# A trunk of two layers: where the norm's steps stand beside the split of weights and the conditioning work

## The chip, the cores and the metric

One Trainium2 chip, one of its cores. The metric is the device time of one execution in microseconds (us), the median of several runs. The kernel is written in Python on a layer that takes the instructions in the order in which the program issues them, keeps one in-order queue for each engine, and sets all semaphores. The order on an engine is made by that layer's scheduler: of the instructions whose operands and buffers are free by its own estimate, the one issued first by the program goes first. That order is then fixed.

## The reference

The input x has 256 tokens of 2048 values, in float32. Two residual layers follow. In each, a vector c gives six vectors of 2048 (shift, scale and gate for the mixer; the same for the MLP), by a product with a matrix of 2048 x 12288 (adaLN).

```python
for l in range(DEPTH):                                   # DEPTH = 2
    mod = silu(c) @ ada_w[l] + ada_b[l]
    shift1, scale1, gate1, shift2, scale2, gate2 = jnp.split(mod, 6, axis=-1)
    h = _modulate(_rms(x, norm1_g[l]), shift1, scale1)   # h * (1 + scale) + shift
    mix = _even_mixer(h, ...) if l % 2 == 0 else _mla_mixer(h, ...)
    x = x + gate1[:, None, :] * mix
    h = _modulate(_rms(x, norm2_g[l]), shift2, scale2)
    x = x + gate2[:, None, :] * (jnp.square(jax.nn.relu(h @ mlp_w1[l])) @ mlp_w2[l])
```

Layer 0's mixer joins a gated spatial mix and a convolution, and ends in a projection of 2048 x 2048. Layer 1's is a low-rank attention with 16 heads: its input projection has 512 columns for the queries' low rank, 512 for keys and values, and 64 for a shared rotary key; it too ends in a projection of 2048 x 2048. The MLP's matrices are 2048 x 8192 and 8192 x 2048.

## The kernel before, in words

**Tokens and products.** The 256 tokens are two halves of 128, h = 0 and 1. `self.x[h]` holds a half's residual. A product takes the activations as stationary operand, transposed (128 values by 128 tokens), and the weights as moving operand, 512 columns at a time, in float32 split into a high part and a low part: three matmuls for each block of 128 rows (high x high, high x low, low x high). A weight tile is 4 blocks by 512 columns, 1 MB. `wraw` loads it on SyncE's queue into one of four `raw` buffers; `wtile` lets ScalarE cast it to the high part `wh` (three buffers) and VectorE subtract to get the low part `wl` (two buffers) (L94, L95). `gemm_part` runs one tile, half 0 and then half 1 (L183 to L185). With `skew`, `gemm` runs the last two tiles of a product as a pair, all of half 0 ahead of half 1. Products whose input comes from a norm at the MLP go by quarters of the input, four blocks each: `gemm_quarter` and `unit_halves` (L210 to L212) run three column blocks ("units") for one quarter while the norm makes the next; for the first quarter the first two units go as a pair, half 0 of both first.

**The norm.** `residual` adds the gated product to x (L411, L412) and lets ScalarE sum the squares (L340). `x_rstd` turns the sum into 1/rms with some ten operations on one value per token (L345 to L90). `norm_t` scales a quarter of x by it into `xn` (L354) and transposes it on TensorE (L107). `norm_quarter` lets ScalarE scale and shift the transposed blocks into `full` (L380) and VectorE split them into `h_h` (L382) and `h_l` (L383). `norm_start` computes `x_rstd` for both halves before the first quarter. The attention's norm (`norm_mod`) makes all four quarters ahead of its products, and those run by columns: 320, 256 and then 512.

**Conditioning.** The adaLN products of 1 x 2048 by a matrix run on VectorE, beside the rest. They are a queue of steps, each with a 1 MB load through the same four `raw` buffers. A step of a row or a column has one VectorE operation (L297, L237); a step of `ada_quarters` has four (L267, L269). `side_work` is called for each weight tile and takes steps at a rate given with them (`R0` to `R6`, `RA`); with `self.hold` set it takes none. `ada_until` takes steps until a condition holds. After layer 0's mixer has begun, the shift and scale of layer 0's MLP are such a queue: 32 steps in four quarters of eight, the first quarter done by the time of the mixer's output projection; the first four of the other 24 go at rate 2.5, the rest at 0.8 per tile.

**The three places of the change.** At the end of layer 0's mixer (`even`) the output projection's fourth block of columns is an ordinary `gemm`, and side work goes on. At the ends of layer 0's MLP and of the attention, `at_end` sets the pair and the hold. In the attention and in layer 1's MLP `self.first = 2`: the low parts of the first two weight tiles are made by GpSimd instead of VectorE (L95 under POOL). In layer 0's MLP that isn't so, and the hold is off from the start.

`tc.issue_after(ins)`, used before in `even`, lets each instruction of its block that is on `ins`'s engine stand behind `ins` in that engine's order; it adds no semaphore and binds no other engine.

## Time and profile before

| what | value |
|---|---|
| median of 3 runs | 2177.03 us (2175.73 to 2178.15) |
| the profiled execution | 2179.71 us, of which the span of the trace is 2178.0 us |
| TensorE busy | 2081.9 us, 9138 matmuls |
| VectorE busy | 1565.5 us |
| ScalarE busy | 930.8 us |
| GpSimd busy | 147.1 us |
| read from HBM | 564.06 MB |
| mean granted TensorE clock | 0.986 |

Times in the profile count from the start of the span. PE is TensorE's matmuls, DVE VectorE, ACT ScalarE, POOL GpSimd, SPq the instructions that SyncE issues. "out<-in" names the program's tiles, xN counts merged instructions, and a bracket gives the idle time before an instruction with what ended it. In the view by stretches the columns are the stretch, its length, the busy time (and number of instructions) of PE, PE's weight loads, DVE, ACT and POOL, the granted clock, the DMAs' busy share, and GB/s.

### The profile page before, as it was taken

Reading aid. Unit: us, or ns where it says so; the run is one execution under the profiler, and the core shown is the slowest. Engines: PE = TensorE matmul, PEld = TensorE weight load, DVE = VectorE, ACT = ScalarE, POOL = GpSimd, SP = SyncE. Lnnn points to the kernel's source line nnn. Section 1 sums busy time; section 2 is a strip of 40 time slices with the busy share of each in tenths; the row PEclk is TensorE's granted clock in tenths of the full one; section 3 lists DMA queues with packets and bytes.
Section 4 is the critical chain, followed back from the end, with each engine's and each line's share of the span. In section 5 each row is a group of like instructions: output and inputs, shape, how many; then the busy total and the mean of one; then the engine's idle time right before and its main releaser. Section 6 shows DMA issues by size and latency. Waiting matters only on the chain.

```text
span 2178.0 us, 23665 instructions
## 1 busy us (share of the span) xinstructions
PE 2081.9 (96%) x9138; PEld 1633.3 (75%) x9138; DVE 1565.5 (72%) x1763; ACT 930.8 (43%) x1184; POOL 147.1 (7%) x95
## 2 busy tenths in 40 slices
PE   2889999799999999999998999989999999999999
PEld 1344458678888888888888888868888888888887
DVE  6849999888777878878667878766656544554555
ACT  2135435344444334334445687444434433433432
POOL 0038710000000000000001000010000000000000
PEclk9999999899999999999999999989999999999999
DMA  9999978799899899989754756747777556556653
GB/s 349 384 351 325 335 248 289 272 316 335 303 337 328 316 322 328 331 309 342 275 178 155 237 163 231 244 140 255 262 270 263 180 191 187 185 192 193 192 190 121
DMA packets 238620, 567.70 MB, mean 261 GB/s; under 512 B 9150, under 2 KB 17784, under 8 KB 221864
## 3 DMA queue, kind: packets, MB, share of 16 engines
q1 hardware_dynamic: 236288, 562.60, 74.5%
q10 hardware_dynamic: 1564, 2.28, 0.3%
q8 instruction: 72, 1.18, 0.2%
q0 software_dynamic: 656, 1.31, 0.2%
q14 instruction: 40, 0.33, 0.0%
HBM read 564.06 MB, written 2.10 MB: 260 GB/s over the span
## 4 chain that ended last, share of the span: by engine, by line
PE 81%; DVE 10%; DMA 5%; ACT 2%; issue 1%; POOL 0%; SPq 0%; ACTq 0%; DVEq 0%; POOLq 0%
PE mm L183 22%; PE mm L185 22%; PE mm L184 22%; PE mm L153 4%; DMA raw<-in_ada_w 3%; PE trp L107 3%; DVE accq L269 3%; DVE wl L95 2%; DVE cvsq L542 1%; PE mm L211 1%; PE mm L210 1%; PE mm L212 1%; DMA raw<-in_mlp_w 1%; DMA raw<-in_ab_w_out 1%; ACT wh L94 1%
## 5 line engine op out<-in xcount | busy, mean ns | idle before, releaser
L95 DVE TENSOR_TENSOR wl<-raw,wh 128x2048 fp32r<-128x2048 f32 (+2 forms) x312 | 704.8, 2259 | 420.8 <-PE mm L184 318.4
L94 ACT CAST wh<-raw 128x2048 fp32r<-128x2048 f32 (+3 forms) x316 | 596.5, 1888 | 779.8 <-PE mm L185 533.0
L183 PE MATMUL mm<-wh,f_h 128*128 128x512 f32 x1024 | 399.6, 390 | 0.0
L185 PE MATMUL mm<-wh,f_l 128*128 128x512 f32 x1024 | 399.3, 390 | 0.0
L184 PE MATMUL mm<-wl,f_h 128*128 128x512 f32 x1024 | 398.7, 389 | 0.0
L185 PE MATMUL mm<-wh,h_l 128*128 128x512 f32 (+2 forms) x928 | 358.4, 386 | 0.0
L183 PE MATMUL mm<-wh,h_h 128*128 128x512 f32 (+2 forms) x928 | 358.2, 386 | 0.0
L184 PE MATMUL mm<-wl,h_h 128*128 128x512 f32 (+2 forms) x928 | 357.0, 385 | 0.6 <-DVE wl L95 0.6
L185 PEld LDWEIGHTS mm<-wh,f_l 128*128 128x128 f32 x1024 | 192.2, 188 | 40.0
L184 PEld LDWEIGHTS mm<-wl,f_h 128*128 128x128 f32 x1024 | 192.3, 188 | 39.8
L183 PEld LDWEIGHTS mm<-wh,f_h 128*128 128x128 f32 x1024 | 192.2, 188 | 39.0
L184 PEld LDWEIGHTS mm<-wl,h_h 128*128 128x128 f32 x928 | 175.0, 189 | 34.2 <-DVE wl L95 1.1
L185 PEld LDWEIGHTS mm<-wh,h_l 128*128 128x128 f32 x928 | 174.9, 189 | 33.3
L183 PEld LDWEIGHTS mm<-wh,h_h 128*128 128x128 f32 x928 | 175.0, 189 | 32.7
L153 PE MATMUL mm<-raw,x 128*128 128x512 f32 x448 | 198.1, 601 | 1.1 <-ACT x L500 0.6
L269 DVE SCALAR_TENSOR_TENSOR accq<-raw,cT,accq 128x512 f32<-128x512 f32 x210 | 153.9, 750 | 16.0 <-DMA raw<-in_ada_w 12.8
L153 PEld LDWEIGHTS mm<-raw,x 128*128 128x128 f32 x448 | 85.4, 193 | 106.4 <-issue 99.5
L237 DVE SCALAR_TENSOR_TENSOR acc<-raw,cT,acc 128x2048 f32<-128x2048 f32 x60 | 140.8, 2347 | 9.6 <-DMA raw<-in_ada_w 9.5
L297 DVE SCALAR_TENSOR_TENSOR acc<-raw,cT,acc 128x2048 f32<-128x2048 f32 x48 | 112.7, 2347 | 3.1 <-DMA raw<-in_ada_w 3.0
L542 DVE SCALAR_TENSOR_TENSOR cvsq<-yp,convw,cvsq 128x256 f32<-128x256 f32 x240 | 96.0, 478 | 0.0
L303 POOL TENSOR_TENSOR side<-side 128x1024 f32<-128x1024 f32 x32 | 74.7, 2360 | 19.6 <-ACT side L302 19.6
L452 ACT ACTIVATE relu<-mm 128x512 f32<-128x512 f32 x60 | 35.8, 599 | 91.9 <-PE mm L185 83.6
(270 smaller groups left out, 2231.3 us busy)
## 6 DMA issues: line engine op xcount, KB each, us to landing
raw<-in_mlp_w SPq DMA_DIRECT2D x256, 1024.0 KB, 5.7
raw<-in_ada_w SPq DMA_DIRECT2D x192, 1024.0 KB, 5.2
raw<-in_ab_w_in SPq DMA_DIRECT2D x32, 1024.0 KB, 9.7
raw<-in_ab_w_out SPq DMA_DIRECT2D x16, 1024.0 KB, 7.5
raw<-in_mla_w_out SPq DMA_DIRECT2D x16, 1024.0 KB, 5.0
raw<-in_mla_w_ukv SPq DMA_DIRECT2D x8, 1024.0 KB
raw<-in_mla_w_uq SPq DMA_DIRECT2D x8, 768.0 KB, 4.6
raw<-in_mla_w_in SPq DMA_DIRECT2D x4, 1024.0 KB, 7.3
```

Of the source, the lines that this page charges most:

```text
L94: self.nc.scalar.copy(hi, src)
L95: (engine or self.nc.vector).tensor_tensor(lo, src, hi.bitcast(F32), op=ALU.subtract)
L107: self.nc.tensor.transpose(ps[:w, i * P : i * P + s.shape[0]], s, self.ident[: s.shape[0], : s.shape[0]])
L153: self.nc.tensor.matmul(ps[h], x[:, 4 * g + k, h * P : (h + 1) * P], raw[:, k, :], start=g + k == 0, stop=4 * g + k == KB - 1,)
L183: nc.tensor.matmul(o, a, hi[:, i, :nw], start=first, stop=False)
L184: nc.tensor.matmul(o, a, lo[:, i, :nw], start=False, stop=False)
L185: nc.tensor.matmul(o, b, hi[:, i, :nw], start=False, stop=last)
L237: nc.vector.scalar_tensor_tensor(acc, raw, self.cT[:, kb : kb + 1], acc, op0=ALU.mult, op1=ALU.add)
L269: self.last = nc.vector.scalar_tensor_tensor(acc, raw[:, k, :], c, acc, op0=ALU.mult, op1=ALU.add).ins
L297: nc.vector.scalar_tensor_tensor(acc, raw, c, acc, op0=ALU.mult, op1=ALU.add)
L303: nc.gpsimd.tensor_tensor(acc[:, sl], acc[:, sl], prod, op=ALU.add)
L542: nc.vector.scalar_tensor_tensor(o, y, wk, o, op0=ALU.mult, op1=ALU.add)
```

## The change

For half 0 the norm's first steps get a fixed place, by marks: the instructions that make `xn` ("x"), the last `full` ("f") and `h_l` ("l") of a half and quarter are kept, and `behind` puts other instructions after them on the same engine.

- In the last `residual` before a norm, half 0's 1/rms and its first `xn` and transposes are issued before half 1's residual, which stands behind that `xn`. Half 1's 1/rms stands behind half 0's first `h_l`.
- The splits of the first three weight tiles stand behind marks: the first behind `xn` of half 0, the second behind `full` and `h_l` of half 0, the third behind those of half 1, all of quarter 0. They are issued in four pieces each, and all on VectorE; GpSimd has no split any more.
- Layer 0's MLP takes part: the output projection of layer 0's mixer ends in a pair, and side work is held from its first tile until the first quarter of the MLP's products is issued.
- Steps that `ada_until` takes before quarter q stand behind half 1's `h_l` of quarter q - 1; the first step that `side_work` takes after a quarter's products stands behind that of the quarter after.
- The attention's norm goes by quarters like the MLP's, with two units (320 and 256 columns); the third product of 512 columns takes the other PSUM pool.

```diff
 class Trunk:
+    FIRST = [[("x", 0, 0)], [("f", 0, 0), ("l", 0, 0)], [("f", 1, 0), ("l", 1, 0)]]
...
     def wtile(self, w, k0, nk, n0, nw):
...
-        engine = self.nc.gpsimd if self.first else None
-        self.split(raw[:, :nk, :nw], hi[:, :nk, :nw], lo[:, :nk, :nw], engine)
-        self.first = max(0, self.first - 1)
+        with self.behind(*(self.first[0] if self.first else ())):
+            for i in range(nk) if self.first else (slice(0, nk),):
+                self.split(raw[:, i, :nw], hi[:, i, :nw], lo[:, i, :nw])
+        self.first = self.first[1:]
         self.side_work(nk * nw / 2048)
         return hi, lo
+
+    def behind(self, *marks):
+        stack = ExitStack()
+        for m in marks:
+            stack.enter_context(self.tc.issue_after(self.marks[m]))
+        return stack
...
         while self.ada_queue and self.ada_credit >= 1:
             self.ada_credit -= 1
-            self.ada_queue.pop(0)[1]()
+            with self.behind(*self.late):
+                self.ada_queue.pop(0)[1]()
+            self.late = ()
...
     def norm_start(self, layer, which):
...
-        r = [self.x_rstd(h) for h in range(NH)]
+        r0, first = self.begun or (None, None)
+        self.begun = None
+        r = [r0, None] if r0 is not None else [self.x_rstd(h) for h in range(NH)]
...
             for h in range(NH):
-                yield h, self.norm_t(h, q, r[h]), [(S[:, k : k + 1], A[:, k : k + 1]) for k in range(4 * q, 4 * q + 4)]
+                if r[h] is None:
+                    with self.behind(("l", 0, 0)):
+                        r[h] = self.x_rstd(h)
+                ps = first if first is not None and (h, q) == (0, 0) else self.norm_t(h, q, r[h])
+                yield h, ps, [(S[:, k : k + 1], A[:, k : k + 1]) for k in range(4 * q, 4 * q + 4)]
...
-    def residual(self, ps, gate, c, last, part=None):
+    def residual(self, ps, gate, c, last, part=None, ahead=False):
...
         for h in range(NH):
+            with self.behind(*([("x", 0, 0)] if ahead and h else [])):
...
+            if ahead and h == 0:
+                r = self.x_rstd(0)
+                self.begun = r, self.norm_t(0, 0, r)
...
     def mlp(self, layer, last):
...
-        self.first = 2 if layer == 1 else 0
-        self.hold = self.hold and layer > 0
+        self.first = self.FIRST
...
             if q < 4:
-                self.ada_until(lambda: self.quarters.get((layer, 3), 4) > q)
+                with self.behind(*([("l", 1, q - 1)] if q else [])):
+                    self.ada_until(lambda: self.quarters.get((layer, 3), 4) > q)
                 self.norm_quarter(quarter, q, x)
             if q >= AHEAD:
                 units = [(ps, w1, u * 512, 512) for u, ps in enumerate(started)]
                 self.gemm_quarter(units, x, q - AHEAD, 2 if q == AHEAD else 0)
                 self.hold = False
+                self.late = (("l", 1, min(q, 3)),)
...
     def even(self, layer):
...
-                pss.append(self.gemm(cat, 0, wo, 0, KB, c * 512, 512))
-            self.residual(pss[c], self.mod[layer, 2], c, "norm")
+                pss.append(self.gemm(cat, 0, wo, 0, KB, c * 512, 512, self.at_end(True)))
+            self.residual(pss[c], self.mod[layer, 2], c, "norm", ahead=c == 3)
...
     def odd(self, layer):
...
-        x = self.norm_mod(layer, 0)
-        self.first = 2
-        self.hold = False
+        x = self.act_pair(KB, f"h{layer}0")
+        quarter = self.norm_start(layer, 0)
+        self.first = self.FIRST
...
-        p1 = self.gemm(x, 0, win, 0, KB, QR, 320)
+        p1, p2 = self.psum2(), self.psum2()
+        for q in range(4 + AHEAD):
+            if q < 4:
+                self.norm_quarter(quarter, q, x)
+            if q >= AHEAD:
+                units = [(p1, win, QR, 320), (p2, win, QR + 320, 256)]
+                self.gemm_quarter(units, x, q - AHEAD, 2 if q == AHEAD else 0)
+                self.hold = False
+                self.late = (("l", 1, min(q, 3)),)
...
-        pq = self.gemm(x, 0, win, 0, KB, 0, QR)
+        pq = [self.ms.tile([P, 512], F32, tag="ms", name=f"pq{h}") for h in range(NH)]
+        for g in range(0, KB, 4):
+            self.gemm_part(pq, x, 0, win, 0, g, KB, 0, QR)
```

More of the change, by code (lines that the diff above doesn't have):

```diff
@@ L61, in __init__ @@
         self.hold = False
-        self.first = 0
+        self.first = []
+        self.marks = {}
+        self.begun = None
+        self.late = ()
         self.conv_rate = 10
@@ L90, in rsqrt, with split @@
         nc.vector.scalar_tensor_tensor(out, w, 1.5 * 3 / 8, out, op0=ALU.add, op1=ALU.mult)
-    def split(self, src, hi, lo, engine=None):
+    def split(self, src, hi, lo):
         self.nc.scalar.copy(hi, src)
-        (engine or self.nc.vector).tensor_tensor(lo, src, hi.bitcast(F32), op=ALU.subtract)
+        self.nc.vector.tensor_tensor(lo, src, hi.bitcast(F32), op=ALU.subtract)
     def act_pair(self, nkb, name):
@@ L142, in side_work @@
             self.ada_credit -= 1
-            self.ada_queue.pop(0)[1]()
+            with self.behind(*self.late):
+                self.ada_queue.pop(0)[1]()
+            self.late = ()
         for _ in range(min(self.conv_rate, len(self.conv_queue))):
@@ L198, in gemm_quarter @@
                 self.unit_halves(units[u : u + 1], ws[u:], x, q)
+        if paired == len(units):
+            self.unit_halves(units, ws, x, q)
     def unit_halves(self, units, ws, x, q):
@@ L379, in norm_quarter @@
             for i, (b, a) in enumerate(cols):
-                nc.scalar.activation(full[:, i, :], ps[:, i * P : (i + 1) * P], AF.Identity, bias=b, scale=a)
+                full_i = nc.scalar.activation(full[:, i, :], ps[:, i * P : (i + 1) * P], AF.Identity, bias=b, scale=a)
+            self.marks["f", h, q] = full_i.ins
             sl = (slice(None), slice(4 * q, 4 * q + 4), slice(h * P, (h + 1) * P))
             nc.vector.tensor_copy(hi[sl], full)
-            nc.vector.tensor_tensor(lo[sl], full, hi[sl].bitcast(F32), op=ALU.subtract)
-    def norm_mod(self, layer, which):
-        pair = self.act_pair(KB, f"h{layer}{which}")
-        quarter = self.norm_start(layer, which)
-        for q in range(4):
-            self.norm_quarter(quarter, q, pair)
-        return pair
+            self.marks["l", h, q] = nc.vector.tensor_tensor(lo[sl], full, hi[sl].bitcast(F32), op=ALU.subtract).ins
     def gated(self, src, gate, h, c):
@@ L399, in gated @@
         nc.vector.tensor_tensor(xs, xs, t, op=ALU.add)
-    def residual(self, ps, gate, c, last, part=None):
+    def residual(self, ps, gate, c, last, part=None, ahead=False):
         nc = self.nc
         for h in range(NH):
-            t = self.tmp.tile([P, 512], F32, tag="t512", name="rt")
-            xs = self.x[h][:, c * 512 : (c + 1) * 512]
-            src = ps[h]
-            if part is not None:
-                nc.vector.tensor_tensor(t, src, part(h), op=ALU.add)
-                src = t
-            nc.vector.tensor_tensor(t, src, gate[:, c * 512 : (c + 1) * 512], op=ALU.mult)
-            nc.vector.tensor_tensor(xs, xs, t, op=ALU.add)
-            if last == "norm":
-                self.sum_squares(h, c)
-            elif last == "out":
-                nc.scalar.dma_start(self.t["out"][h * P : (h + 1) * P, c * 512 : (c + 1) * 512], xs)
+            with self.behind(*([("x", 0, 0)] if ahead and h else [])):
+                t = self.tmp.tile([P, 512], F32, tag="t512", name="rt")
+                xs = self.x[h][:, c * 512 : (c + 1) * 512]
+                src = ps[h]
+                if part is not None:
+                    nc.vector.tensor_tensor(t, src, part(h), op=ALU.add)
+                    src = t
+                nc.vector.tensor_tensor(t, src, gate[:, c * 512 : (c + 1) * 512], op=ALU.mult)
+                nc.vector.tensor_tensor(xs, xs, t, op=ALU.add)
+                if last == "norm":
+                    self.sum_squares(h, c)
+                elif last == "out":
+                    nc.scalar.dma_start(self.t["out"][h * P : (h + 1) * P, c * 512 : (c + 1) * 512], xs)
+            if ahead and h == 0:
+                r = self.x_rstd(0)
+                self.begun = r, self.norm_t(0, 0, r)
     def mlp(self, layer, last):
@@ L464, in mlp @@
                 if fb == DFF // FB - 1:
-                    self.residual(ps, self.mod[layer, 5], c, last, (lambda h: y(h, c)) if c < 3 else None)
+                    self.residual(ps, self.mod[layer, 5], c, last, (lambda h: y(h, c)) if c < 3 else None, c == 3 and last == "norm")
                     continue
@@ L860, in odd @@
             ps = self.gemm((oh, ol), 0, wout, 0, KB, c * 512, 512, self.at_end(c == 3))
-            self.residual(ps, self.mod[layer, 2], c, "norm")
+            self.residual(ps, self.mod[layer, 2], c, "norm", ahead=c == 3)
     def setup(self):
```

5 lines of the change are left out of this document (2 added, 3 removed).

## The prediction

> **What bounds the kernel now.** First the page: busy time, then the chain that ended last.
>
> ```profile
> span 2178.0 us, 23665 instructions
> PE 2081.9 (96%) x9138; PEld 1633.3 (75%) x9138; DVE 1565.5 (72%) x1763; ACT 930.8 (43%) x1184; POOL 147.1 (7%) x95
> ...
> PE 81%; DVE 10%; DMA 5%; ACT 2%; issue 1%; POOL 0%; SPq 0%; ACTq 0%; DVEq 0%; POOLq 0%
> ```
>
> TensorE is busy 96% of the span and carries 81% of the chain. No matmul is removed, so only time in which TensorE waits or runs at a low clock can go. The stages view (busy time by stretch; the clock stands ahead of the DMA share) shows where that is after the start: at the three hand-overs from a residual to the next norm.
>
> ```profile
> 410.00:420.00 10.00, 2.40 (x12) 1.69 (x11) 9.10 (x27) 5.05 (x6) 0.00 (x0) 0.72 1.01 355
> 450.00:460.00 10.00, 10.00 (x45) 8.28 (x45) 10.00 (x13) 1.92 (x1) 0.00 (x0) 1.00 0.77 247
> 480.00:490.00 10.00, 8.26 (x29) 6.29 (x29) 8.06 (x5) 5.00 (x5) 0.00 (x0) 0.83 0.97 370
> 1150.00:1160.00 10.00, 5.76 (x26) 4.50 (x24) 8.87 (x13) 3.25 (x4) 5.80 (x2) 0.93 0.31 76
> 1440.00:1450.00 10.00, 1.87 (x9) 1.21 (x7) 9.83 (x7) 3.04 (x2) 8.18 (x2) 0.76 0.43 120
> 1450.00:1460.00 10.00, 7.84 (x28) 6.29 (x29) 8.01 (x20) 5.73 (x16) 0.00 (x0) 0.55 0.23 92
> ```
>
> TensorE runs 45 matmuls in a full 10 us (the 450 us row): 0.222 to 0.227 us each, I use 0.225. At 410, 1150 and 1440 us (layer 0's MLP, the attention, layer 1's MLP) TensorE works 2.4, 5.8 and 1.9 of 10 us, and the clock falls as well. In layer 0 VectorE and the DMAs are near full in the same stretch (9.1 of 10 us, share 1.01); at 1440 us the DMAs have room (0.43). That difference decides my sum. The timeline of layer 1's MLP:
>
> ```profile
> 1438.67 0.16 DVE L345 TENSOR_REDUCE v<-ssq 128x1 f32<-128x4 f32 x1 [0.79 <-ACT junk L340]
> 1439.15 9.04 POOL L95 TENSOR_TENSOR wl<-raw,wh 128x2048 fp32r<-128x2048 f32 x2 [35.51 <-PE mm L185]
> 1439.24 4.51 DVE L79 SCALAR_TENSOR_TENSOR nr<-r,v 128x1 f32<-128x1 f32 x1
> ...
> 1441.48 0.39 PE L185 MATMUL mm<-wh,o_l 128*128 128x512 f32 x1
> ...
> 1443.78 4.42 DVE L87 SCALAR_TENSOR_TENSOR nr<-nr 128x1 f32<-128x1 f32 x1
> ...
> 1450.71 1.09 PE L107 MATMUL trp<-ident,xn 128*128 128x128 f32 x4 [8.85 <-DVE xn L354]
> ...
> 1450.96 0.16 DVE L345 TENSOR_REDUCE v<-ssq 128x1 f32<-128x4 f32 x1 [0.39 <-ACT junk L340]
> 1451.53 0.22 DVE L79 SCALAR_TENSOR_TENSOR nr<-r,v 128x1 f32<-128x1 f32 x1
> ...
> 1452.61 0.48 DVE L354 TENSOR_SCALAR xn<-x,r 128x512 f32<-128x512 f32 x1
> 1453.38 0.43 DVE L382 CAST h_h<-full 128x512 fp32r<-128x512 f32 x1 [0.28 <-ACT full L380]
> 1453.98 0.78 PE L210 MATMUL mm<-wh,h_h 128*128 128x512 f32 x1
> ```
>
> The last attention matmul ends at 1441.48 + 0.39 = 1441.87; the first MLP matmul starts at 1453.98: 12.1 us. In the first rsqrt two one-element steps take 4.51 and 4.42 us while GpSimd makes the first two low parts (9.04 us); in the second rsqrt, with GpSimd idle, the same L79 takes 0.22. Whatever the mechanism, the first half's chain loses 8.5 us to GpSimd's work.
>
> **The change, part by part.** Prices: VectorE's groups between 412 and 461 us (busy us, then mean ns of one), and the page's row of adaLN loads (KB, us to landing).
>
> ```profile
> L269 DVE SCALAR_TENSOR_TENSOR accq<-raw,cT,accq 128x512 f32<-128x512 f32 x27 | 19.6, 750 | 0.1
> L95 DVE TENSOR_TENSOR wl<-raw,wh 128x2048 fp32r<-128x2048 f32 x6 | 13.8, 2292 | 2.6 <-PE mm L211 1.6 <-ACT wh L94 0.9
> L383 DVE TENSOR_TENSOR h_l<-full,h_h 128x512 fp32r<-128x512 f32 x6 | 4.1, 687 | 0.0
> ...
> raw<-in_ada_w SPq DMA_DIRECT2D x192, 1024.0 KB, 5.2
> ```
>
> *Low parts to VectorE, the first half's norm ahead (layer 1's MLP).* Undisturbed, the chain from the sum (1450.96) to xn (1452.61) takes 1.65 us. From 1438.67 that puts xn at 1440.3 to 1440.8, before the last matmul. The transposes then start at 1441.9. From transposes to first matmul it is 1453.98 - 1450.71 = 3.3 us; that is with transposes at the half clock (1.09 us), so less is possible; but ScalarE may take the other half's square first. I take 3.3: first matmul at 1445.2, gain 8.8 (bounds: 7.5, and 12.1 if nothing were left).
>
> What the gain must pay. Each of the first two low parts now costs VectorE four pieces, 2.3 to 2.8 us by the L95 and L383 rows (2.29 whole, 4 x 0.69 in pieces); the first lies in its wait for transposes and ScalarE (3.3 us), costing nothing; uncovered it would be 2.8 at most. The second half's rsqrt, before done ahead of the first matmul, now stands behind the first half's low part: 0.69 + 1.65 + 0.48, up to 2.8 of second-tile pieces between, then 3.3 to its matmul: 6 to 9 us, against 24 matmuls of the first half (5.4) plus their half-clock time (1.7). I charge 1.0. The second tile's casts now wait behind ScalarE's modulate of the first half; TensorE has 12 matmuls (2.7 us) before it needs them: covered, at most 1 if not. The second half's residual now waits for xn, which is ready (1440.8) before that half's last matmul: no cost. The half clock: before, TensorE ran from 1453.98 to about 1459 at 0.55; the new idle is shorter, and I charge one low stretch of 3.4 us (the 480 us row: clock 0.83 in 10 us behind a short wait) against about 5, worth +1.0. Net: 8.8 - 1.0 + 1.0 = **8.8 us gained**, bounds 6 and 11.
>
> *The attention.* Same construction, smaller.
>
> ```profile
> 1152.85 2.73 DVE L79 SCALAR_TENSOR_TENSOR nr<-r,v 128x1 f32<-128x1 f32 x1
> ...
> 1155.25 0.51 PE L793 MATMUL sc<-mask,identr 128*128 128x384 f32 x2
> ...
> 1164.21 0.61 PE L183 MATMUL mm<-wh,h_h 128*128 128x320 f32 x1
> ...
> 1197.03 0.28 PE L185 MATMUL mm<-wh,h_l 128*128 128x256 f32 x1
> ```
>
> TensorE is free at 1155.25 + 0.51 = 1155.8 and restarts at 1164.2, 8.4 us. With 3.3 it restarts at 1159.1: 5.1 gained. The two projections (320 and 256 columns) now go together by quarter, the same 192 matmuls; but the first half of a quarter is only 24 short matmuls (1164.2 to 1197.3 for 192 and the work between: 0.17 each at most), 4.1 together, so the second half, 6 us behind, is waited for: -1.9; the half clock costs as before. The third projection's accumulators move to other banks, and its loads stay in place: nothing, covered by matmuls on both sides; two mask matmuls (0.51) fall behind it: the same work later. **3.2 gained**, bounds 0.5 and 5.5.
>
> *Layer 0's MLP: the norm ahead, and work held back.* Here the hand-over is alike:
>
> ```profile
> 398.61 0.63 PE L107 MATMUL trp<-ident,accq 128*128 128x128 f32 x4 [1.35 <-DVE accq L269]
> ...
> 404.32 0.69 DVE L221 TENSOR_REDUCE mod<-trp 128x4 f32<-128x512 f32 x1
> ...
> 411.90 0.39 PE L185 MATMUL mm<-wh,cat_l 128*128 128x512 f32 x1
> ...
> 419.89 0.45 PE L107 MATMUL trp<-ident,xn 128*128 128x128 f32 x1 [7.60 <-DVE nr L87]
> ...
> 423.24 0.79 PE L210 MATMUL mm<-wh,h_h 128*128 128x512 f32 x1 [2.26 <-DVE h_h L382]
> ...
> 432.71 0.69 DVE L383 TENSOR_TENSOR h_l<-full,h_h 128x512 fp32r<-128x512 f32 x1
> ...
> 440.25 5.81 SPq L118 DMA_DIRECT2D raw<-in_ada_w  x3
> ...
> 450.17 0.37 SPq L118 DMA_DIRECT2D raw<-in_mlp_w  x1
> ...
> 452.87 5.39 DVE L269 SCALAR_TENSOR_TENSOR accq<-raw,cT,accq 128x512 f32<-128x512 f32 x8
> ...
> 461.51 0.47 PE L210 MATMUL mm<-wh,h_h 128*128 128x512 f32 x1
> ...
> 499.92 0.40 PE L212 MATMUL ms<-wh,h_l 128*128 128x512 f32 x1
> ```
>
> 412.3 to 423.2 is 10.9 us. The last output projection becomes paired, so its first half ends 24 matmuls (5.4 us) ahead instead of 12, and side work is held. The adaLN transposes and the wait before them (398.61: 1.35 + 0.63, and a second four) leave this projection; it ends near 410, and the first MLP matmul comes near 413.5: 9.7 earlier.
>
> But the held work is needed soon. The queue holds 24 adaLN steps for this norm after the mixer (a 1 MB load and four VectorE operations each); from its rates (2.5 for four, then 0.8 a tile) 13 are done before the last projection and 16 after: the reduce at 404.32 closes the sixteenth. Now steps 14 to 16 wait for the first group of tiles and for the second half's low part of quarter 1; they, 17 and 18, and 19 to 24 must pass before quarter 3's norm, and on the load queue quarter 2's first tile comes behind step 24. That order is visible: three loads at 440.25, then the tile's at 450.17; steps to 458.3; its matmuls at 461.51.
>
> The first quarter's two halves plus quarter 1's take about 12 us from the first matmul (before: 423.2 to 433.4, the second half's rsqrt already done), so steps may begin at 426. From there to quarter 2's first low part: 44 operations of 0.67 (5.39 / 8, overlapped) to 0.75 us = 29.6 to 33.0; four low parts, 8.8 to 9.2; a norm quarter, 2 x (0.48 + 0.43 + 0.69) = 3.2; two reduces 1.5. Together 43 to 47: quarter 2 starts at 469 to 473, I take 470, against 461.5, although TensorE would be ready near 450 (two quarters of 72 x 0.225, transposes and a low-clock stretch from 413.5). From there before took 500.3 - 461.5 = 38.8; now the loads are ahead: 2 x 72 x 0.225 = 32.4, 16 transposes at half of 1.09 for four 2.2, one low-clock stretch 1.7: 36.3, end 506.3. **6.0 us lost**, bounds 16 lost and 8.5 gained (next part). Steps that follow are paced by tiles and fall due later: no cost. On SyncE's queue three adaLN loads fall behind the MLP's first tiles, which come sooner for it; GpSimd's queue only loses work; at both layer-1 stages the side work was held before as well, and nothing is queued anew.
>
> *Sum.* 2179.71 (the profiled execution) - 8.8 - 3.2 + 6.0 = 2173.7. That execution lies 2.7 above the median 2177.03, so I predict **2171.0 us**. Outside these stages every matmul keeps its place, so the shift lasts to the end.
>
> **The rivals.**
>
> *Short gaps keep the clock.* The 480 us row speaks against it: TensorE lacks only 1.7 us there, and the clock went to 0.83. If gaps of some 2 us leave it at 1.0, the low stretches (1.7 each) go: 2166. The Trainium skill, "TensorE: Matmul & The Clock Gate", Part 1, states that the clock halves after at least one idle window of about 3.4 us, and by that the new gaps would keep it. By that rule the sum would be 2166; the 480 us row disagrees with it.
>
> *The backlog is hidden.* If quarter 2's tiles get past the late steps, quarter 3 alone waits, near 481 (before: in the 480 us row), ending at 499: 1 gained, 2164; with VectorE's gaps used as well nearly the whole lead stays, 8.5 gained: 2156.5. For it: the DMAs stand at 0.77 in the 450 us row. Against: the load order above, and VectorE at 10.00 in the same row.
>
> *The second halves come late.* If the pieces, the square and the rsqrt of the second half get in each other's way for 2.5 to 3 us more at both layer-1 stages, those bring 6 and 0.5: 2176.5, no change.
>
> *Slower: the backlog waits for loads.* A load takes 5.2 us from issue to landing and there are four buffers. If a step costs 4 to 5 us instead of 2.9, quarter 2 starts at 482 to 493, the loss is 18 to 29, and the time 2183 to 2194. It decides from 3.8 us a step on (a loss above 16.4 cancels 12.0 and the 0.2%). Against it: 1 MB at the 370 GB/s of the 480 us row is 2.8 us.
>
> **How the numbers follow.** 0.2%, about what a measurement tells from no change, is 4.4 us: faster is below 2172.7. Chances: forecast 0.45 (its own range 2166 to 2176), clock kept 0.08, backlog hidden 0.19, second halves late 0.16, slower 0.12. Faster: 0.35 of the forecast, 0.08 and 0.19: 0.62. Same: 0.10 and 0.16: 0.26. Slower: 0.12. The range 2158 to 2179 leaves out the slower case and the end of the hidden one.
>
> **What would show it.** In the new trace: no GpSimd operation at both layer-1 hand-overs, each rsqrt step about 0.2 us, xn of the first half before the last matmul; from last to first matmul 3 to 4 us at all three; then in layer 0 TensorE idle some 15 to 20 us before quarter 2, behind adaLN steps, and quarter 2's first matmul near 470. If TensorE starts quarter 2 before 462, the step on the backlog is wrong and the time nearer 2158; if the layer-1 gaps stay above 6 us, the steps on the chain are.

## The result, and the profile after

The change makes the kernel slower by 0.65%: 2191.56 us (median of 6 runs, 2189.63 to 2196.11) against 2177.59 (6 runs, 2175.73 to 2180.19) on the same chip, a ratio of 1.0065, 95% interval 1.0054 to 1.0075. The forecast was 2171.0. The profiled executions differ by 11.7 us (spans of 2189.7 and 2178.0), the medians by 14.0; the stages below are of the former. The page of the changed kernel, its span, busy times and the shares of the chain that ended last:

```profile
span 2189.7 us, 23705 instructions
...
PE 2085.0 (95%) x9138; PEld 1634.1 (75%) x9138; DVE 1562.8 (71%) x1794; ACT 932.3 (43%) x1211; POOL 132.4 (6%) x91
...
PE 84%; DVE 9%; DMA 4%; ACT 2%; issue 1%; SPq 0%; ACTq 0%; DVEq 0%
```

The page can't tell what happened: the same 9138 matmuls, VectorE no busier, 11.7 us more span. So the span is cut where TensorE's last matmul of each stage ends (read from the timeline of each kernel; us):

| kernel | layer 0's mixer ends | layer 0's MLP | attention | layer 1's MLP |
|---|---|---|---|---|
| before | 412.3 | 743.1 | 286.5 | 731.5 |
| after | 410.5 | 759.8 | 289.8 | 725.1 |
| after less before | -1.8 | +16.7 | +3.3 | -6.4 |

Those four differences are the 11.7 us, within rounding.

**Layer 0's MLP.** First the view by stretches, of before and then of after (columns as in the prediction):

```profile
390.00:400.00 10.00, 8.65 (x41) 6.92 (x40) 9.78 (x12) 2.53 (x3) 0.00 (x0) 1.00 0.72 241
400.00:410.00 10.00, 10.00 (x47) 8.14 (x46) 9.93 (x14) 3.83 (x2) 0.00 (x0) 1.00 1.00 362
420.00:430.00 10.00, 7.74 (x30) 6.15 (x31) 7.58 (x18) 4.51 (x12) 0.00 (x0) 0.60 0.64 208
```

```profile
390.00:400.00 10.00, 10.00 (x46) 8.29 (x45) 5.00 (x5) 3.68 (x5) 0.00 (x0) 1.00 0.66 190
400.00:410.00 10.00, 10.00 (x46) 8.29 (x45) 5.62 (x15) 2.56 (x6) 0.00 (x0) 1.00 0.42 145
410.00:420.00 10.00, 5.22 (x16) 3.97 (x16) 7.64 (x21) 4.18 (x10) 0.00 (x0) 0.71 0.31 107
420.00:430.00 10.00, 10.00 (x49) 8.17 (x49) 7.58 (x15) 6.37 (x16) 0.00 (x0) 0.94 0.32 105
...
460.00:470.00 10.00, 1.12 (x4) 0.72 (x4) 9.68 (x15) 0.00 (x0) 0.00 (x0) 0.60 1.03 377
470.00:480.00 10.00, 6.52 (x20) 5.06 (x21) 7.28 (x11) 3.41 (x5) 1.80 (x1) 0.54 0.97 348
480.00:490.00 10.00, 8.06 (x30) 5.95 (x29) 7.79 (x7) 7.00 (x7) 0.00 (x0) 0.83 0.66 208
...
1460.00:1470.00 10.00, 5.13 (x16) 3.34 (x14) 7.64 (x22) 4.18 (x10) 0.00 (x0) 0.83 0.41 117
```

From 390 to 430 us VectorE was busy for 36.4 of 40 us before (with the 9.10 of the row shown in the prediction) and for 25.8 after; the DMAs moved 11.7 MB and now 5.5. From 460 us on TensorE all but stands still (1.12 of 10, the granted clock at half from 462.1 to 479.2) while the other two catch up. How much they have to catch up, in VectorE's groups of instructions (count, busy us, mean ns), from 427.1 us to each kernel's own start of quarter 2, of after and then of before:

```profile
L286 DVE SCALAR_TENSOR_TENSOR accq<-raw,cT,accq 128x512 f32<-128x512 f32 x42 | 29.8, 747 | 0.5
...
L284 DVE TENSOR_SCALAR accq<-raw,cT 128x512 f32<-128x512 f32 x2 | 1.0, 478 | 0.0
```

```profile
L269 DVE SCALAR_TENSOR_TENSOR accq<-raw,cT,accq 128x512 f32<-128x512 f32 x19 | 13.6, 750 | 0.1
```

44 operations for 19: 17.2 us of VectorE that lay before 427 and now lie behind it. The timeline of after:

```profile
408.91 0.49 DVE L371 TENSOR_SCALAR xn<-x,r 128x512 f32<-128x512 f32 x1
...
410.29 0.60 PE L112 MATMUL trp<-ident,xn 128*128 128x128 f32 x4
...
415.67 0.80 PE L227 MATMUL mm<-wh,h_h 128*128 128x512 f32 x1 [4.78 <-DVE h_h L406]
...
444.09 16.47 SPq L123 DMA_DIRECT2D raw<-in_ada_w  x6
...
453.33 16.57 DVE L286 SCALAR_TENSOR_TENSOR accq<-raw,cT,accq 128x512 f32<-128x512 f32 x23
...
462.43 0.37 SPq L123 DMA_DIRECT2D raw<-in_mlp_w  x1
...
468.50 1.12 PE L112 MATMUL trp<-ident,accq 128*128 128x128 f32 x4 [9.71 <-DVE accq L286]
...
470.56 1.90 ACT L99 CAST wh<-raw 128x2048 fp32r<-128x2048 f32 x1 [20.02 <-DMA raw<-in_mlp_w]
...
473.62 1.20 PE L227 MATMUL mm<-wh,h_h 128*128 128x512 f32 x2
```

`xn` is ready ahead of the last matmul and TensorE starts the MLP 7.6 us earlier than before (423.24). Then 23 adaLN operations run without a break, quarter 2's first tile stands in the load queue behind the loads of six adaLN steps (it is issued at 462.43, and ScalarE can cast it at 470.56), and TensorE waits 9.71 us. Quarter 3 ends at 514.65; before it was 500.31.

**The attention.** Its hand-over shrank from 8.8 to 4.6 us, and the third projection (the queries') starts 38.4 us after the MLP's end (41.7 before). Behind it, in the timeline of after:

```profile
1233.63 0.16 DVE L684 TENSOR_SCALAR rss<-rss 128x2 f32<-128x2 f32 x1
...
1233.84 2.35 DVE L254 SCALAR_TENSOR_TENSOR acc<-raw,cT,acc 128x2048 f32<-128x2048 f32 x1
...
1237.68 0.75 DVE L694 TENSOR_SCALAR lxn<-pq,rr 128x512 f32<-128x512 f32 x1
1238.34 2.28 DVE L100 TENSOR_TENSOR wl<-raw,wh 128x2048 fp32r<-128x2048 f32 x1
1240.54 0.74 DVE L694 TENSOR_SCALAR lxn<-pq,rr 128x512 f32<-128x512 f32 x1
...
1241.34 1.11 PE L112 MATMUL trp<-ident,lxn 128*128 128x128 f32 x4 [2.03 <-DVE lxn L694]
```

`rss` is the queries' sum of squares and `lxn` their scaled values. An adaLN step of 2.35 us stands between the sum and its rsqrt, and the split of a weight tile (2.28 us) has come between the two halves' `lxn`. TensorE waits 3.0 us for `lxn` in two waits, the granted clock is at half from 1240.3 to 1247.2, and the eight pairs of heads (from the end of the third projection to the start of the output projection) take 126.2 us instead of 118.3.

**Layer 1's MLP** gained 6.4. Its hand-over:

```profile
1458.45 0.49 DVE L371 TENSOR_SCALAR xn<-x,r 128x512 f32<-128x512 f32 x1
...
1459.83 0.60 PE L112 MATMUL trp<-ident,xn 128*128 128x128 f32 x4
...
1462.58 0.63 ACT L357 ACTIVATE junk<-x 128x512 f32<-128x512 f32 x1 [5.82 <-DVE x L430]
...
1463.21 1.49 ACT L403 ACTIVATE full<-trp,mod,A 128x128 f32<-128x128 f32 x4
...
1465.21 0.50 PE L227 MATMUL mm<-wh,h_h 128*128 128x512 f32 x1 [4.78 <-DVE h_h L406]
```

The transposes are done at 1460.4, yet ScalarE begins the modulate at 1463.21: half 1's square stands ahead of it in ScalarE's queue and waits for half 1's residual. Between last and first matmul lie 5.2 us (12.1 before).

### The profile page after: what moved, and what is told of

It reads as the page before. It is cut to its first block, busy times and chain, and to the rows that moved or that the text cites. A ratio compares the mean times of both kernels' runs of the same rounds, so it can differ in the third digit from the quotient of the medians.

```text
span 2189.7 us, 23705 instructions
## 1 busy us (share of the span) xinstructions
PE 2085.0 (95%) x9138; PEld 1634.1 (75%) x9138; DVE 1562.8 (71%) x1794; ACT 932.3 (43%) x1211; POOL 132.4 (6%) x91
## 3 DMA queue, kind: packets, MB, share of 16 engines
q10 hardware_dynamic: 1564, 2.28, 0.3%
## 4 chain that ended last, share of the span: by engine, by line
PE 84%; DVE 9%; DMA 4%; ACT 2%; issue 1%; SPq 0%; ACTq 0%; DVEq 0%
PE mm L198 22%; PE mm L199 22%; PE mm L200 22%; PE mm L168 5%; DMA raw<-in_ada_w 4%; DVE accq L286 3%; PE trp L112 3%; DVE wl L100 2%; DVE cvsq L564 1%; PE mm L229 1%; PE mm L228 1%; PE mm L227 1%; PE ms L227 1%; PE ms L229 0%; PE ms L228 0%
## 5 line engine op out<-in xcount | busy, mean ns | idle before, releaser
L100 DVE TENSOR_TENSOR wl<-raw,wh 128x2048 fp32r<-128x2048 f32 (+3 forms) x343 | 714.5, 2087 | 422.2 <-PE mm L199 318.0
L198 PE MATMUL mm<-wh,h_h 128*128 128x512 f32 x832 | 326.3, 392 | 0.0
L200 PE MATMUL mm<-wh,h_l 128*128 128x512 f32 x832 | 325.8, 392 | 0.0
L199 PE MATMUL mm<-wl,h_h 128*128 128x512 f32 x832 | 324.4, 390 | 0.0
L200 PEld LDWEIGHTS mm<-wh,h_l 128*128 128x128 f32 x832 | 156.2, 188 | 32.2
L199 PEld LDWEIGHTS mm<-wl,h_h 128*128 128x128 f32 x832 | 156.3, 188 | 31.8
L198 PEld LDWEIGHTS mm<-wh,h_h 128*128 128x128 f32 x832 | 156.3, 188 | 31.2
L227 PE MATMUL mm<-wh,h_h 128*128 128x512 f32 (+2 forms) x192 | 73.2, 385 | 16.4 <-DVE h_h L406 13.7
```

What stands on the lines that cost most here:

```text
L100: self.nc.vector.tensor_tensor(lo, src, hi.bitcast(F32), op=ALU.subtract)
L198: nc.tensor.matmul(o, a, hi[:, i, :nw], start=first, stop=False)
L199: nc.tensor.matmul(o, a, lo[:, i, :nw], start=False, stop=False)
L200: nc.tensor.matmul(o, b, hi[:, i, :nw], start=False, stop=last)
L227: nc.tensor.matmul(o, a, hi[:, i, :nw], start=k == 0, stop=False)
```

## The experiments

All ran as single kernels on one chip per group; a ratio is to the kernel before on that chip. Stage times in us are from each kernel's one profiled execution. Layer 1's MLP as changed is in eleven of them; ten took 724.7 to 727.8 and att_credit 730.1, so a stage is good to some 2 us. The profiled execution of mlp1_only lies 5.2 us above the median of its five runs. The expectations count from before's 2177.6 us; where a group's median of before was another, a ratio times 2177.6 is the fair number.

| kernel | ratio, 95% interval | mixer ends | layer 0's MLP | quarter 2 starts, quarter 3 ends | attention (heads) | layer 1's MLP |
|---|---|---|---|---|---|---|
| before | 1 | 412.3 | 743.1 | 461.5, 500.3 | 286.5 (118.3) | 731.5 |
| after | 1.0065, 1.0054 to 1.0075 | 410.5 | 759.8 | 473.6, 514.7 | 289.8 (126.2) | 725.1 |
| l0_hold_off | 0.9967, 0.9955 to 0.9979 | 412.4 | 740.7 | 458.4, 498.9 | 282.5 (118.5) | 726.0 |
| l0_undone | 0.9979, 0.9970 to 0.9988 | 410.3 | 743.2 | 460.1, 497.0 | 282.0 (118.6) | 727.8 |
| mlp1_only | 0.9960, 0.9946 to 0.9974 | 412.5 | 744.3 | 463.0, 501.7 | 283.5 (118.0) | 725.5 |
| att_credit | 1.0095, 1.0080 to 1.0110 | 410.9 | 758.8 | 473.6, 515.7 | 288.3 (124.8) | 730.1 |
| att_entry | 1.0041, 1.0027 to 1.0055 | 410.1 | 762.4 | 473.5, 515.2 | 282.8 (118.5) | 726.4 |
| half_ops | 1.0016, 1.0005 to 1.0026 | 411.0 | 751.1 | 470.0, 507.8 | 289.4 (126.0) | 724.7 |
| half_loads | 1.0045, 1.0030 to 1.0060 | 409.7 | 757.5 | 469.9, 513.1 | 286.7 (123.5) | 726.5 |
| half_both | 1.0009, 0.9998 to 1.0020 | 410.8 | 753.3 | 469.6, 506.0 | 288.7 (124.8) | 725.0 |
| tile_first2 | 1.0056, 1.0039 to 1.0072 | 409.4 | 756.7 | 456.9, 512.5 | 290.2 (126.2) | 724.8 |
| tile_first_half | 1.0024, 1.0013 to 1.0036 | 409.2 | 752.8 | 458.8, 507.2 | 288.6 (124.7) | 724.8 |
| sq_behind | 0.9934, 0.9920 to 0.9947 | 411.9 | 739.7 | 455.7, 497.6 | 281.0 (118.6) | 725.9 |
| hold_later | 0.9933, 0.9920 to 0.9945 | 412.2 | 739.0 | 456.8, 496.9 | 280.7 (118.6) | 722.2 |
| pieces | 0.9938, 0.9924 to 0.9951 | 411.1 | 744.1 | 458.5, 500.1 | 279.9 (118.5) | 722.4 |
| pieces_l0_undone | 0.9934, 0.9922 to 0.9947 | 410.5 | 743.4 | 460.3, 498.9 | 279.9 (118.6) | 721.8 |

**Which part loses.** l0_hold_off takes one thing out of the changed kernel:

```diff
-                pss.append(self.gemm(cat, 0, wo, 0, KB, c * 512, 512, self.at_end(True)))
+                pss.append(self.gemm(cat, 0, wo, 0, KB, c * 512, 512, True))
```

> The changed kernel without one thing: in layer 0 the adaLN steps are no longer held back while the last output projection and the MLP's first tiles run. The first half's norm still has its fixed place, the last two tiles are still paired, the first tiles' low parts still come in pieces. Theory A (the loss is the hold): VectorE stood at 5.0 and 5.6 of 10 us and the DMAs at 190 and 145 GB/s in the two stretches from 390 us, and what was left out there came back in front of quarter 2; without the hold quarter 2 starts before 465 us (now 473.6), the layer 0 MLP's quarters end near 500 (now 514.5), and since the side work's credit at the attention's start is then 0.25 again instead of 0.40, no adaLN step falls into the query's rsqrt: 2160 to 2168 us. Rival B (the fixed places and the pairing themselves cost it): quarters still end after 510 us, and only the attention changes: 2183 to 2188 us. Rival C (neither, the two losses are of other causes): within 3 us of 2191.6.

Its stretches:

```profile
400.00:410.00 10.00, 9.90 (x46) 7.71 (x45) 8.78 (x14) 4.81 (x7) 0.00 (x0) 1.00 1.01 367
410.00:420.00 10.00, 5.59 (x21) 4.09 (x20) 9.67 (x28) 4.20 (x11) 0.00 (x0) 0.82 0.64 230
420.00:430.00 10.00, 8.78 (x38) 6.84 (x38) 8.26 (x21) 3.61 (x11) 0.00 (x0) 0.84 0.77 259
```

Theory A holds in each stage it named (quarter 2 at 458.4, quarter 3's end at 498.9, heads 118.5); the time, 0.9967 of before or 2170.4, is 2 us above its range and far from B's. VectorE and the DMAs are at work through the hand-over, and the hand-over is as short as with the hold (417.4 less 412.4, 5.0 us; 5.2 with it): the hold is not what makes the chain quick. What it brings is an earlier end of the mixer, by some 1.4 us on average: 409.2 to 411.0 in the eight kernels with the hold, 410.3 to 412.5 in the eight without. The attention is right as well without being touched. l0_undone takes layer 0's part back whole (`ahead`, the pair, the marks and the hold), and mlp1_only the attention's part too:

> The changed kernel with layer 0's part taken back whole: no hold, no pairing, no fixed place and whole low parts at layer 0's MLP; the attention and layer 1's MLP as changed. Theory A: layer 0's MLP loses its 14.8 us; the attention, with its credit at 0.25, keeps the 3.3 us that it has gained when the query projection starts and loses none of the 7 us after; layer 1's MLP keeps 6.9: 2177.6 - 3.3 - 6.9 = 2167.4 us, 2164 to 2171. Rival D (the attention's own loss of 7 us comes from its new order of projections or the query's accumulators in the other banks, not from where the side work falls): the attention still ends 3.8 us later than before, relative to its start: 2177.6 + 3.8 - 6.9 = 2174.5 us.

> Layer 1's MLP alone as changed (first half's norm ahead, fixed places, low parts in pieces on VectorE); layer 0 and the attention as before, except that the attention's first two low parts are on VectorE too, in whole tiles and with no fixed place. If the terms are independent: 2177.6 - 6.9 = 2170.7 us for the MLP, and at the attention up to 2.7 us more from the rsqrt step that no longer takes 2.73 us: 2168 to 2171. If the MLP's gain in the changed kernel was helped by what came before it, above 2173.

By its ratio l0_undone is at 2173.0, outside A's range and nearer to D's 2174.5 than to A's 2167.4; the stage decides between the two, 282.0 for the attention and not 290. mlp1_only, at 2168.9, is where it was expected: its MLP gained 6.0, and the attention 3.0, where all that differs from before is that the first two splits run on VectorE and no longer on GpSimd beside the first half's rsqrt (the step of 2.73 us on L79 and one of 2.81 on L87 take 0.22 and 0.16 there). So of the 3.7 to 4.5 that the attention gains in the kernels with its part and a credit of 0.25 (l0_hold_off, l0_undone, att_entry), about 3 seem to need no new order at all; with a stage good to some 2 us, this is one profile's figure.

**Why the attention lost.** Two tries at the side work's credit (a number that grows with each weight tile; a step is taken when it passes 1). By the program's own count it is 0.25 at the attention's start before, and 0.40 with the hold in layer 0. att_credit raises it by 0.425 after the paired projections, att_entry lowers it by 0.15 at the start:

> The changed kernel with one number more: after the attention's paired projections the side work's credit is raised by 0.425, so that the steps fall after the same tiles of the query projection as before; the work and its amount stay. Layer 0 keeps its loss. Theory A': no 2.35 us adaLN step between the query's squares and its rsqrt (now at 1233.8 us), the transposes for both halves come within 6 us of the projection's end (now 9.4), the attention gains about 6 to 7 us: 2191.6 - 6.5 = 2185 us, 2183 to 2187. Rival D (the order of projections or the banks cost it): the step moves and the attention stays as long, within 2 us of 2191.6.

> The changed kernel with one number more: the side work's credit is lowered by 0.15 at the attention's start, from 0.40, which the hold in layer 0 has left, to the 0.25 that it has without the hold. Layer 0 keeps its loss. VectorE's order in the attention is then that of the kernel without the hold. Theory A'' (the attention's loss is where the steps fall in its heads, and that is set by the credit): the attention takes 282.5 us as it does without the hold (289.8 as changed), the heads 118.5 (126.2): 2191.6 - 7.3 = 2184 us, 2182 to 2187. Rival D' (what slows the heads is the later side work's amount or the memory traffic after a late layer 0): heads stay above 123 us, 2189 to 2196.

The first missed: by its ratio 2198.3 us, above both ranges. The rsqrt was freed (the first matmuls of the queries' second projection came 6.7 us after the third projection's end, as before, against 10.0), but the heads still took 124.8 us, with one wait alone of 2.53 us at 1333.4. So the step in the rsqrt is not the whole of the loss; that the other steps fell badly is argued from this. The second gave 118.5 and 282.8, as l0_hold_off has, and by its ratio 2186.5, in its range. In its timeline only the rsqrt's own operations, of 0.16 to 0.17 us each, stand between VectorE's sum of squares and `lxn`:

```profile
1236.51 0.16 DVE L684 TENSOR_SCALAR rss<-rss 128x2 f32<-128x2 f32 x1
...
1238.29 1.41 DVE L694 TENSOR_SCALAR lxn<-pq,rr 128x512 f32<-128x512 f32 x2
```

So the new order of projections and the other banks cost nothing that the stage shows; 0.15 more in a counter, left by the hold a whole MLP earlier, cost 7 us.

**What paces the refill in layer 0.** The changed kernel with half of the VectorE operations, half of the loads, or both, in the 11 late steps alone. The lines are those of half_both; half_ops changes the last of them only, half_loads the load only, and its four operations read the loaded half twice:

```diff
+            less = layer == 0 and j0 == 3 and 8 * q + 2 * g + i >= 21
-            raw = self.wraw(self.t["ada_w"][layer], 4 * g, 4, (j0 + i) * D + q * 512, 512)
+            raw = self.wraw(self.t["ada_w"][layer], 4 * g, 2 if less else 4, (j0 + i) * D + q * 512, 512)
-            for k in range(4):
+            for k in range(2 if less else 4):
```

> The changed kernel, with only two of the four VectorE operations in each of the 11 adaLN steps of layer 0 that the hold leaves for the MLP; their loads stay whole. (Half of their products are left out.) VectorE has 22 operations less of 0.72 us, 16 us. Theory V (VectorE sets the pace of the refill): quarter 2's first matmul comes 12 to 16 us earlier, near 460 (now 473.6), and the time is 2191.6 - 12 to 16 = 2176 to 2180 us. Theory L (the loads set it: 377 GB/s in the stretch from 460 us): quarter 2 starts after 470, 2188 to 2191. Both at once: near 466, 2183 to 2186.

> The changed kernel, with only half of each load (512 KB for 1024) in the same 11 adaLN steps; all four VectorE operations stay and read the loaded half twice. (The second half of the products is replaced.) 5.8 MB less, at 377 GB/s 15.3 us of the DMAs. Theory V: quarter 2's first matmul still after 470, 2188 to 2191 us. Theory L: near 460, 2176 to 2180. Both at once: near 466, 2183 to 2186.

> The changed kernel, with both halvings: in the 11 late adaLN steps of layer 0 two of four VectorE operations and half of each load. (Half of their products are left out.) With half the operations alone quarter 2 started at 470.0 and ended at 491.4, VectorE at 6.8 and 6.4 of 10 us and the DMAs at 370 and 397 GB/s; with half the loads alone it started at 469.9, VectorE at 10.00 twice. If the refill is bound by the two together and by nothing else, quarter 2 starts at 456 to 461, quarter 3 ends at 495 to 501 (before: 500.3), and layer 0's MLP takes 740 to 745 us: 2174 to 2178 us. If something else of the hold (the tiles parked in the load buffers, the order of loads) is left, quarter 2 starts after 465 and the time is above 2181.

The stretches from 450 to 470 us of half_ops, and then of half_loads:

```profile
450.00:460.00 10.00, 10.00 (x46) 8.29 (x45) 6.79 (x8) 0.00 (x0) 0.00 (x0) 1.00 1.02 370
460.00:470.00 10.00, 3.75 (x16) 2.48 (x15) 6.39 (x12) 1.95 (x2) 1.44 (x1) 0.72 1.04 397
```

```profile
450.00:460.00 10.00, 7.40 (x33) 5.76 (x31) 10.00 (x14) 0.00 (x0) 0.00 (x0) 1.00 0.67 206
460.00:470.00 10.00, 1.26 (x5) 0.86 (x5) 10.00 (x17) 1.90 (x1) 0.00 (x0) 0.58 0.85 278
```

VectorE looks like the tighter of two bounds that lie close together: without half of its work quarter 3 ends 6.9 us earlier, and then the DMAs are full (share 1.02 and 1.04); without half of the loads 1.5 us, with VectorE at 10.00. No one theory's number came out, and both halvings together gave 8.6 and not the whole. What was left looked like the place of quarter 2's first tile in the load queue, behind six adaLN loads (half_both, SyncE's queue):

```profile
442.36 14.17 SPq L123 DMA_DIRECT2D raw<-in_ada_w  x6
...
457.88 0.37 SPq L123 DMA_DIRECT2D raw<-in_mlp_w  x1
```

So quarter 2's first tiles (two in tile_first2, one in tile_first_half, where both are halved) were loaded ahead:

```diff
-        raw = self.wraw(w, k0, nk, n0, nw)
+        raw = self.early.pop(0) if self.early else self.wraw(w, k0, nk, n0, nw)
...
+                if layer == 0 and q == 3:
+                    self.early = [self.wraw(w1, 8, 4, u * 512, 512) for u in range(2)]
                 with self.behind(*([("l", 1, q - 1)] if q else [])):
                     self.ada_until(lambda: self.quarters.get((layer, 3), 4) > q)
```

> The changed kernel with its hold, and quarter 2's first two tiles loaded and split ahead of the last adaLN steps: on the load queue they pass five adaLN loads, on VectorE 18 operations; no work is left out. Theory O (a part of the loss is that the tiles stand behind the late steps, in the load queue and on VectorE): quarter 2 starts at 459 to 464 us (now 473.6), its first 48 matmuls run under the steps, and quarter 3, which needs the last step, ends at 501 to 507 (now 514.65): 2191.6 - 8 to - 13 = 2179 to 2184 us. Rival P (the end is set by the last step alone, quarter 3's norm): quarter 2 starts early, but quarter 3 ends after 511, 2188 to 2191.

> The kernel with half the operations and half the loads in the late steps (so half of their products are left out), and quarter 2's first tile ahead of five of the adaLN loads. With the two halvings quarter 2 still started at 469.63 and quarter 3 ended at 506.0, since its first tile was issued behind six adaLN loads, at 457.88. Theory O: quarter 2 at 458 to 463, quarter 3's end at 497 to 502, layer 0's MLP 743 to 748 us (753.3), and with that all of the loss is accounted for. If quarter 3 still ends after 505, something of the hold is left that neither the operations, the loads nor this order explains.

Theory O fell. Quarter 2 starts at 456.9 and 458.8, as early as it could, and quarter 3 ends only 2.1 us earlier in the one and no earlier in the other: TensorE's wait moves behind the last step (5.61 us at 468.4 in tile_first2, and the clock halves for 20.5 us from 472.4). Rival P is right for the most part: the last step sets the end, whatever runs ahead of it. One more queue stands on the way: ScalarE casts quarter 2's remaining tiles behind quarter 3's modulate, which waits for the last step (ScalarE is idle for 20.06 us ahead of it in tile_first2 and for 16.56 in tile_first_half), and TensorE then waits 4.8 us for these tiles in either, most of it at the half clock (3.1 us in l0_hold_off, at full clock). No run moved these casts, so what they cost is not shown. Without the hold layer 0's loss is gone (shown). Halving VectorE's late operations gives back 6.9 of the 14.3 us (shown); halving the loads 1.5, which is less than a stage is good to; the other 6 us stay unassigned.

**What was left of the hand-over.** On l0_hold_off, the square of half 1 behind half 0's modulate on ScalarE; then, in hold_later, layer 1's hold kept until the norm's four quarters are made; then, in pieces, the first cast in four parts; last, pieces with layer 0's part taken back:

```diff
                 if r[h] is None:
+                    with self.behind(("f", 0, 0)):
+                        self.sum_squares(h, 3)
                     with self.behind(("l", 0, 0)):
                         r[h] = self.x_rstd(h)
...
-                if last == "norm":
+                if last == "norm" and not (ahead and h):
                     self.sum_squares(h, c)
...
-                self.hold = False
+                self.hold = layer == 1 and q < 4
...
+            for i in range(4) if (h, q) == (0, 0) else (slice(0, 4),):
```

> The kernel without layer 0's hold, and one more edit: ScalarE's square of the second half now has its place behind the modulate of the first half, at all three hand-overs. In the changed kernel the first half's transposes end at 1460.43, but ScalarE begins the modulate at 1463.21, because the square stands ahead of it in its queue and waits for the second half's residual (1461.86 + 0.69). Theory E (that queue is what is left of the hand-over): modulate from 1460.5, its 1.49 us, the cast, the first matmul at 1462.5 instead of 1465.2: 2.7 us less at the attention and at layer 1's MLP, gaps 1.9 and 2.5; at layer 0 the start comes as much earlier but the end is set by VectorE, 0 to 1: 2167.5 - 5.4 to - 6.4 = 2161 to 2162 us, 2159 to 2164. Rival F (the first matmul is then early, but waits for the tiles' pieces or the second half's chain, which no longer starts sooner): gaps shorter, but stages as long: 2166 to 2168 us.

> The kernel with the square behind the modulate, and in layer 1's MLP the side work is held until all four quarters of the norm are made, not until the first quarter's matmuls. There TensorE waited 2.36 us at 1476.1 for xn, which stood in VectorE's queue behind an adaLN step that waited 4.65 us for its load, and the clock went to half for 3.4 us. There is time for the held steps later: VectorE is at 5 of 10 us there, and nothing waits for them before the end. If that is what stopped it: no such wait, 2164 - 2.4 - 1.7 = 2160 us, 2158 to 2162. If the steps only stop another operation later, as in the attention: 2163 to 2165.

> The same as hold_later, and the first half's first quarter is cast and subtracted in four pieces of 128 columns, each right behind its part of the modulate. The first matmul needs the first piece alone. Idle of TensorE at the three hand-overs now 2.62, 2.06 and 2.50 us after the transposes; the modulate's four parts take 1.49 us, of which three (1.1) need no longer be waited for: 1.6, 1.0 and 1.4 us, below the 1.8 to 2.0 us of idle in a 3.4 us window from which the clock was lowered in the traces so far. At the attention and layer 1's MLP 1.1 each, and 1.7 where a half-clock stretch goes: 2160 - 2.2 to - 4 = 2156 to 2158 us. If VectorE's eight small operations delay what follows: 2159 to 2162.

> The same as pieces, with layer 0's part taken back whole (layer 0's MLP as in the kernel before). Theory G (what layer 0's early start gains is taken back by VectorE, which stands at 9.7 to 9.9 of 10 us from 430 to 460 us, so the end of quarter 3 stays near 497 to 500 either way): 0 to 2.5 us slower than pieces. Rival H (a hand-over of 10.8 us cut to 4 or less is worth its 6 us where nothing is held): 5 to 7 us slower than pieces.

The timeline of sq_behind at layer 1's MLP:

```profile
1433.09 1.50 ACT L405 ACTIVATE full<-trp,mod,A 128x128 f32<-128x128 f32 x4 [3.71 <-PE trp L112]
...
1435.26 0.63 ACT L357 ACTIVATE junk<-x 128x512 f32<-128x512 f32 x1 [0.16 <-DVE x L432]
...
1435.56 0.50 PE L227 MATMUL mm<-wh,h_h 128*128 128x512 f32 x1 [2.50 <-DVE h_h L408]
...
1473.13 2.35 DVE L314 SCALAR_TENSOR_TENSOR acc<-raw,cT,acc 128x2048 f32<-128x2048 f32 x1 [4.65 <-DMA raw<-in_ada_w]
...
1478.47 0.66 PE L112 MATMUL trp<-ident,xn 128*128 128x128 f32 x4 [2.36 <-DVE xn L371]
```

The modulate now follows the transposes and the hand-over is 2.9 us, as Theory E says. At 2163.2 by its ratio the kernel is in E's range, but the attention gained 1.5 us where 2.7 were expected, and layer 1's MLP gained nothing: TensorE waits later for an `xn` that stands behind an adaLN step waiting for its load. With that hold kept longer (hold_later) layer 1's MLP came to 722.2, 3.7 less; the ratio did not move (0.9933 after 0.9934, 2163.0 us where 2158 to 2162 was expected), so this gain is the profile's alone. Pieces was expected at 2156 to 2158 and is at 2164.1: the hand-overs of layer 1 shrink again (2.1 and 1.5 us), the attention by 0.8, and the ratio shows nothing of it. And pieces_l0_undone is as fast as pieces: Theory G. With nothing held, layer 0's early start is worth nothing that these runs show (a hand-over of 2.4 us against 11.2, and layer 0's MLP at 744.1 against 743.4), since quarter 3 ends near 499 to 500 either way.

hold_later and pieces_l0_undone are at 2162.08 and 2162.06 us (5 runs each) against 2176.84, faster than both kernels; sq_behind and pieces can't be told from them.

## Why the prediction was wrong, step by step

In the profiled executions 6.0 us were to be gained and 11.7 were lost. Of the 17.7 us between, 8.8 are layer 0's, 6.5 the attention's and 2.4 those of layer 1's MLP.

- **Layer 0: 6.0 us lost was forecast, 14.3 measured at quarter 3's end, 14.8 at the MLP's.** The mechanism was right: 44 operations came behind 427 us, and quarter 2's first tile came behind the late steps on the load queue. The term was mis-sized, in two places. "I take 470" was 3.6 short (473.62). The rest, "36.3, end 506.3", took 41.0: the half clock lay on quarter 2's matmuls from 473.6 to 479.2 and from 486.0 to 489.4, at most 4.5 us lost by these times where one stretch of 1.7 was charged, and TensorE waited 1.48, 0.88 and 1.06 us for quarter 2's three tiles, which the sum took as loaded ahead. The runs assign about half of the 14.3 us to the late VectorE operations; the other half stays open. And the sum paid for something that the hold doesn't bring: of the 7.6 us by which the MLP starts earlier (9.7 forecast), 5.9 come without the hold (417.37 in l0_hold_off). For the rest VectorE gives up 10.6 us of work (36.4 less 25.8 of the 40 us above), which comes back behind 427 us.
- **The attention: 3.2 gained was forecast, 3.3 lost measured.** The hand-over's part was right (38.4 for 41.7, 3.3 gained). The step that failed is "nothing is queued anew", with "Steps that follow are paced by tiles and fall due later: no cost". The hold moves the counter's remainder, and with it each later step; att_entry takes that shift back and the loss is gone.
- **Layer 1's MLP: 8.8 gained was forecast, 6.4 measured** (3.7 to 6.8 in ten of the kernels that share it), about the low bound of 6. From `xn` to transposes it went as forecast. The 3.3 us from transposes to first matmul were 5.4: half 1's square went first on ScalarE, which the text named and did not price. In the trace of after it is half 1's residual (done at 1461.86 + 0.69) and the square; the modulate starts 2.8 us after the transposes' end.
- **The signs it named.** No split on GpSimd, rsqrt steps of 0.22 us at most, and `xn` ahead of the last matmul came as said. The hand-overs took 5.2, 4.6 and 5.2 us, not 3 to 4, and TensorE was idle for 12.1 us (9.71 and 2.38) ahead of quarter 2, not 15 to 20.
- **The rivals.** "Slower: the backlog waits for loads" gave 2183 to 2194 and the time lies there, but not by its mechanism: a step cost 2.9 us (16.57 for 23 operations), not 4 to 5, and halving the loads gave 1.5 us. That the time fell into this rival's range is luck. "The backlog is hidden" has its condition in tile_first2, where quarter 2's tiles do get past the late steps, and there quarter 3 ends at 512.5, not at 499; the 498.9 of l0_hold_off comes from having no backlog. "The second halves come late" is near for layer 1's MLP (6.4 for its 6), where the second half's square did get in the way, but of the first half's modulate; at the attention's hand-over it isn't so. "Short gaps keep the clock" is refuted below, for gaps that put 1.95 us or more into one window.

## What to carry to other kernels

Put the few operations of a critical chain at a fixed place and leave the rest running. Here a hold brought no shorter hand-over, and in a stage where VectorE was busy for 9 of 10 us the held work was paid back later, with waits on top. When background work is paced by a counter, any change to it upstream moves every later step; look in the new order of each engine for a long step that has landed inside a short chain. After a chain is shortened on one engine, follow it into the next in-order queue: here the modulate stood behind a square that waited.

## What the runs showed of the hardware

**The clock is judged in windows, by a share.** In all 16 traces the granted clock changes at steps of 3.413 us. I counted TensorE's idle time in each such window at full clock from 125 us on: of 74 windows with 1.95 us idle or more, 73 were followed by the half clock; of 42 with 1.5 to 1.95, 16; of some 9200 with less, none ahead of the program's end. In sq_behind the gap of 2.50 us at 1433.1 was split by a boundary (1.95 and 0.5) and the clock stayed; the gap of 2.36 at 1476.1 lay in one window and the clock fell. The Trainium skill, "TensorE: Matmul & The Clock Gate", Part 1, states that the window is free-running, which the traces bear out, and that the clock halves after at least one idle window; there the measurement decides: a window a little over half idle is enough. The Trainium skill, "TensorE: Matmul & The Clock Gate", Part 4, says of transposes that they don't count as busy in the same way; in the count they are taken as busy, and it separates better so: with them as idle 33 of 111 windows of 1.95 us or more kept the clock. Whether these float32 transposes run in the mode that the page means, no run here shows.

**GpSimd next to one-element work.** In the kernel before, two steps of the first half's rsqrt on one value per token, L79 and L87, took 4.51 and 4.42 us beside GpSimd's split of 9.04 us at layer 1's MLP, and 2.73 and 2.81 us beside one of 5.80 at the attention. No split ran on GpSimd in any of the new kernels, and the same two steps (L84 and L92 of the kernel after) took 0.22 and 0.16 us in each hand-over.
